# Tile starts modulo 64 bytes, chosen for each use, in a two-layer trunk

## The chip, the core and the metric
The kernel runs on one core of one Trainium2 chip. The metric is the time of one execution on the device in microseconds (us), smaller being better. TensorE multiplies matrices: it loads one operand as weights (stationary) and streams the other through (moving). VectorE (DVE) and ScalarE (ACT) work element by element, and SyncE (SP) issues the transfers (DMA) from the chip's memory into SBUF, the on-chip memory of 128 partitions. A tile is a block of SBUF: so many bytes in each partition, from a start address that is the same in all of them.

## The reference, cut to what matters
A trunk of two layers over 256 tokens of width 1024. Each layer has four blocks with a residual: a feed-forward block, four gated mixers, cross-attention to a memory of 256 tokens, and a second feed-forward block.

```python
def swiglu(h, w_in, w_out):
    a, b = jnp.split(h @ w_in, 2, axis=-1)
    return (jax.nn.silu(a) * b) @ w_out

for l in range(DEPTH):                                   # 2
    h = rms_norm(x, ffn1_pre_g[l])
    x = x + 0.5 * rms_norm(swiglu(h, ffn1_w_in[l], ffn1_w_out[l]), ffn1_post_g[l])
    h = rms_norm(x, mix_pre_g[l])
    u_conv, u_pool, q_nsa, kv_nsa, g_nsa, q_swa, kv_swa, u_gate = jnp.split(h @ w_in[l], splits, axis=-1)
    ...                                                  # four mixers: y_a, y_b, y_c, y_d
    merged = gates[:, :, 0] * (y_a @ w_branch[l, 0])
    for n in range(1, N_BRANCH):
        merged = merged + gates[:, :, n] * (branches[n] @ w_branch[l, n])
    x = x + rms_norm(merged @ w_out[l], mix_post_g[l])
    h = rms_norm(x, x_pre_g[l])
    x = x + rms_norm(cross_attention(h, rms_norm(mem, mem_g[l]), w_xq[l], w_xkv[l], w_xo[l]), x_post_g[l])
    h = rms_norm(x, ffn2_pre_g[l])
    x = x + 0.5 * rms_norm(swiglu(h, ffn2_w_in[l], ffn2_w_out[l]), ffn2_post_g[l])
```

## The kernel before
Every weight goes through the core once, as chunks of 1 MB (128 x 2048 numbers of 4 bytes) in a fixed order: per layer 22 chunks `f1i` and 11 `f1o` for the first feed-forward block; then the mixers' projections `qn`, `kva`, `kvb`, `pool`, `conv`, `qs`, `kvs`, gates `g0` to `g3` and branches `b0` to `b3`, and `wo`; then `xk`, `xq`, `xv`, `xo`; then `f2i` and `f2o`. `_fetch` (L303) loads a chunk in two halves into `raw` and splits each into a rounded part `hi` (ACT, L266) and a rest `lo` (DVE, L269). Activations are split in the same way, and each product is three matmuls (`mm3`, L282: high x high, high x low, low x high), all recorded on L280.

Two forms of product occur. With the weights stationary (`ws`), activations of 256 tokens stream through 128 weight columns at a time: the feed-forward input from its fourth chunk on, gates, branches, `xk`, `xq`. With the activations stationary (`xs_rows`, `tok_part`), the weights stream through: 512 columns in the feed-forward output, `wo`, `xv`, `xo`, `qn`, `kva` and `qs`, 280 in `kvb`, and 256 in `kvs` and in the first three chunks of each feed-forward input. A chunk of 512 columns makes 2 token tiles x 2 column halves x 2 row blocks x 3 products = 24 matmuls.

A chunk mostly goes into the pools `hi` and `lo` (four buffers of 4096 bytes each). At some places a chunk goes whole into other tiles that are free just then, its spares (`use_spare`, L326): `hT_spare` gives the tiles of hT (traced as `hwh`, `hwl`), `y_spare` those of y (`yw`), and two lambdas those of the mid pool (`sph`, `spl`) and of kT (`sp`). In each feed-forward block the spares serve its chunk 2 (y), and of the eleven output chunks the ninth (hT), tenth (y) and eleventh (mid pool). In the mixers, y serves the first half of `kva`; kT serves the last chunk of `wo`. `xs_rows` holds the last two or four chunks and goes through them once for each token tile.

hT (`hTh`, `hTl`) holds the normalised activations of the block that runs. The y tiles hold branch inputs (`ypair`, read by `branch_chunk`), then the merged sums `mh`, `ml` for `wo` (made in `mixer`), then the queries of the cross-attention. `mid` holds the feed-forward block's inner activations, `A` the normalised memory (`Ah`, `Al`) and then the attention's output `oT`.

Pools lie one behind the other. `phase` (L241) puts tiles of 32 bytes between groups of pools. In the program built from this kernel the tiles start at these remainders modulo 64 bytes:

| tiles | start modulo 64 |
|---|---|
| `hi`, `lo` | 0 |
| hT (and its spare; the attention's `pT`) | 32 |
| y (and its spare) | 32 |
| `mid` and the mid pool's spare | 0 |
| `Ah`, `Al`, `oT`, kT (and its spare), `xv` | 0 |

Slices taken from a tile (columns, tokens, row blocks) begin at multiples of 512 bytes in it, so they keep its remainder; those of `kvb` are 1120 bytes apart and alternate. Modulo 128, y is at 96 and hT at 32; `hi`, `lo`, `mid` and the mid pool's spare are at 0 (modulo 512, `hi` and `lo` are at 256, `mid` and the mid pool's spare at 0).

The order of the instructions comes from the order in the code, with priorities (`front`, `urgent`) and a planner that places work by its own estimates.

Of the kernel before, what the change touches and what calls it, by code (L numbers as in the profile page):

```python
# [8 lines left out]
F32R = mybir.dt.float32r  # L9
# [6 lines left out]
P = 128  # L16
D = 1024
S = 256
L = 2
NT = 2  # L20
KD = 8
# [25 lines left out]
          "x_post_g", "ffn2_pre_g", "ffn2_post_g")  # L47

CW = 2048
FG = 3000  # L50


# [83 lines left out]
def _pack(I):  # L136
    chunks = []
    for l in range(L):
        ch = {nm: iter(c) for nm, c in _layer_chunks(I, l).items()}
        for nm, n in _ORDER:  # L140
            for _ in range(n):
                a = next(ch[nm])
                if a.shape[1] < CW:
                    a = np.pad(a, ((0, 0), (0, CW - a.shape[1])))
                chunks.append(a)
# [61 lines left out]
class Trunk:  # L207
# [95 lines left out]
    def _fetch(self, pos):  # L303
        if pos >= len(self.plan) or pos in self.ready:
            return
        nm = self.plan[pos]
        n = 1120 if nm == "kvb" else CW
        with ExitStack() as ctx:
            for i in self.behind.pop(pos, ()):
                ctx.enter_context(self.tc.issue_after(i))  # L310
            ctx.enter_context(self.tc.high_priority(offset=FG))
            big = self.spare.pop(pos)() if pos in self.spare else None
            halves = []
            for i in range(2):
                if big is not None:
                    hi, lo = (b[:, i * n // 2:(i + 1) * n // 2] for b in big)
                else:
                    hi, lo = (p.tile([P, CW // 2], F32R, tag=t, name=t)[:, :n // 2]
                              for p, t in ((self.hip, "hi"), (self.lop, "lo")))
                raw = self.rawp.tile([P, CW // 2], F32, tag="raw", name="raw")  # L320
                self.nc.sync.dma_start(raw[:, :n // 2], self.w_d[pos, :, i * n // 2:(i + 1) * n // 2])
                self.split(hi, lo, raw[:, :n // 2])
                halves.append((hi, lo))
        self.ready[pos] = nm, halves
# [6 lines left out]
            self.early.setdefault(self.cur + at, []).append(self.cur + ahead)  # L331

    def hT_spare(self):
        return [self.hTp.tile([P, CW], F32R, tag="hT" + i, name="hw" + i) for i in "hl"]

    def y_spare(self):
        return [self.yp.tile([P, CW], F32R, tag="y", name="yw") for _ in range(2)]

    def chunk(self, nm, k):
        for pos in [self.cur, self.cur + 1] + self.early.pop(self.cur, []):  # L340
# [11 lines left out]
    def front(self):  # L352
        return self.tc.high_priority(offset=FG)

    def urgent(self):
        return self.tc.high_priority(offset=2 * FG)

    def load(self):  # L360
# [4 lines left out]
        self.x = [self.const.tile([P, D], F32, name="x%d" % t) for t in range(NT)]  # L365
        with self.tc.high_priority(offset=10 * FG):
            for h in range(2):
# [119 lines left out]
        return rs  # L487

    def new_hT(self, pool, tag):
        return [pool.tile([P, KD, S], F32R, tag=tag + i, name=tag + i) for i in "hl"]  # L490

    def pre(self, xs, g, pool, tag):
        hi, lo = self.new_hT(pool, tag)
# [102 lines left out]
    def ffn(self, l, which, h, nxt):  # L596
        nm = "f1" if which == "ffn1" else "f2"
        with self.tc.tile_pool(name="mid", bufs=1) as mp:
            mid = [mp.tile([P, NFF, S], F32R, name="mid%d" % i) for i in range(2)]
            self.use_spare(lambda: [mp.tile([P, CW], F32R, tag="sp" + i, name="sp" + i) for i in "hl"], 32, 28)  # L600
            self.use_spare(self.y_spare, 2)
            self.use_spare(self.y_spare, 31, 26)
            self.use_spare(self.hT_spare, 30, 24)

            def glu(a, b, n=S):
                t, u = self.t2([P, n]), self.t2([P, n])
                with self.front():
                    self.act(t, a, AF.Tanh, scale=0.5)
                    self.stt(u, t, 1.0, a, ALU.add, ALU.mult)
                    self.stt(t, u, 0.5, b, ALU.mult, ALU.mult)  # L610
                return t

            ws = [self.chunk(nm + "i", KD) for _ in range(3)]
            for t in range(NT):
                tok = slice(t * P, (t + 1) * P)
                vs = []
                for c in ((0, 1), (2,)):
                    ps = self.pacc((P, 2, 2, P))
                    calls = [lambda i=i, k=k: self.mm3(
                        ps[:, i - c[0]].rearrange("p a n -> p (a n)"), h[0][:, k, tok], h[1][:, k, tok],  # L620
                        ws[i][0][k], ws[i][1][k], i == c[0] and k == 0, k == KD - 1)
                        for i in c for k in range(KD)]
                    if t == 0 and c[0]:
                        self.behind_turn(calls, 2)
                    else:
                        for call in calls:
                            call()
                    v = glu(ps[:, :len(c), 0, :], ps[:, :len(c), 1, :], len(c) * P)
                    vs += [v[:, i * P:(i + 1) * P] for i in range(len(c))]
                pt = self.ptr((P, 3, P))  # L630
                for i in range(3):
                    self.nc.tensor.transpose(pt[:, i, :], vs[i], self.ident)  # L632
                self.split(mid[0][:, 0:3, tok], mid[1][:, 0:3, tok], pt)
            for i in range(3, NFF):
                w = self.chunk(nm + "i", KD)
                ps = self.pmm()
                self.ws(ps[:, 0, :], w, slice(0, P), h, KD)
                self.ws(ps[:, 1, :], w, slice(P, 2 * P), h, KD)
                v = glu(ps[:, 0, :], ps[:, 1, :])
                with self.front():  # L640
                    self.split(mid[0][:, i, :], mid[1][:, i, :], v)
            gpost = self.gain(which + "_post_g", l)
            gpre = self.gain(nxt[0], nxt[1]) if nxt else None
            hT, then = self.boundary(gpost, True, gpre)
            self.xs_rows(nm + "o", 11, lambda i, k: mid[i][:, k, :], 4, then=then)
        return hT
# [107 lines left out]
    def mixer(self, l, h):  # L754
        nc, tc = self.nc, self.tc
        with tc.tile_pool(name="mix", bufs=1) as mp:
            self.ap = mp
            self._mixer(l, h, mp)
            mg = self.merged
            mh, ml = zip(*[self.ypair() for _ in range(2)])  # L760
            for j in range(4):
                a, s2 = j // 2, slice(2 * (j % 2), 2 * (j % 2) + 2)
                with self.front():
                    self.split(mh[a][:, s2, :], ml[a][:, s2, :], mg[a][:, s2, :], scale=0.5)
        return mh, ml

    def ypair(self):

        y = self.yp.tile([P, 2, 4, S], F32R, tag="y", name="y")
        return [y[:, 0], y[:, 1]]  # L770

    def _mixer(self, l, h, mp):
        nc = self.nc
# [457 lines left out]
    def wo_cross(self, l, mg):  # L1231
        nc, tc = self.nc, self.tc
        with tc.tile_pool(name="cross", bufs=1) as cp:
# [9 lines left out]
            h, then = self.boundary(gpost, False, gpre, False)  # L1243
# [5 lines left out]
            def cols(nm, src, put):  # L1249
                for i in range(4):  # L1250
                    w = self.chunk(nm, KD)
                    ps = self.pmm()
                    for j in range(2):
                        self.ws(ps[:, j, :], w, slice(j * P, (j + 1) * P), src, KD)
                    put(i, ps)
# [10 lines left out]
                self.split(qT[0][a][:, s2, :], qT[1][a][:, s2, :], ps, scale=1.0 / 16)  # L1266

            cols("xq", h, put_q)
            pT = [self.hTp.tile([P, NT, 4, S], F32R, tag="hT" + "hl"[i], name="pT%d" % i) for i in range(2)]
            for hp in range(2):  # L1270
                for t in range(NT):
                    tok = slice(t * P, (t + 1) * P)
                    bank = self.pmm()
                    for j in range(2):
                        for dt in range(2):
                            k = (hp * 2 + j) * 2 + dt
                            a, kk = k // 4, k % 4
                            self.mm3(bank[:, j, :], qT[0][a][:, kk, tok], qT[1][a][:, kk, tok],
                                     kT[0][:, k, :], kT[1][:, k, :], dt == 0, dt == 1)
                    p = self.softmax(bank, 2, S, on_dve=True)  # L1280
# [9 lines left out]
            for hh in range(2):  # L1290
                for t in range(NT):
                    n = slice(hh * 512, (hh + 1) * 512)
                    with self.urgent():
                        self.split(v[0][:, t, n], v[1][:, t, n], acc[t][hh])
            oT = [cp.tile([P, KD, S], F32R, tag="A" + "hl"[i], name="oT%d" % i) for i in range(2)]
            for hd in range(4):
                ps = self.pmm()
                for dt in range(2):
                    n = slice((hd * 2 + dt) * P, (hd * 2 + dt + 1) * P)
# [9 lines left out]
            hT, then = self.boundary(gpost, False, gpre)  # L1309
# [10 lines left out]
def trunk_kernel(tc, x, mem, pos, stream, gains, small, consts, out):  # L1320
    with ExitStack() as ctx:
        k = Trunk(ctx, tc, x, mem, pos, stream, gains, small, consts)
        with tc.high_priority(offset=10 * FG):
            h = k.load()
# [38 lines left out]
```

## Time and profile before

| | us |
|---|---|
| median of 3 runs | 1589.12 |
| lowest and highest | 1588.38, 1589.21 |
| the profiled execution | 1588.27 |
| its span, first to last instruction | 1586.5 |
| TensorE busy in it | 1561.8 |
| DVE, ACT busy | 1148.1, 860.8 |

The profile is of one execution. TensorE's matmuls overlap: each is listed with a start and a modelled length, and the next one starts before the length is over. The distance between two starts is the time that a matmul adds. In the names, `acc<-hi,mid` is a matmul that writes `acc`, streams `hi` and has `mid` loaded as weights; numbers of buffers are left out.

### The profile page before, as it was taken

Reading aid. Unit: us, or ns where it says so; the run is one execution under the profiler, and the core shown is the slowest. Engines: PE = TensorE matmul, PEld = TensorE weight load, DVE = VectorE, ACT = ScalarE, POOL = GpSimd, SP = SyncE. Lnnn points to the kernel's source line nnn. Section 1 sums busy time; section 2 is a strip of 40 time slices with the busy share of each in tenths; the row PEclk is TensorE's granted clock in tenths of the full one; section 3 lists DMA queues with packets and bytes.
Section 4 is the critical chain, followed back from the end, with each engine's and each line's share of the span. In section 5 each row is a group of like instructions: output and inputs, shape, how many; then the busy total and the mean of one; then the engine's idle time right before and its main releaser. Section 6 shows DMA issues by size and latency. Waiting matters only on the chain.

```text
span 1586.5 us, 28413 instructions
## 1 busy us (share of the span) xinstructions
PE 1561.8 (98%) x11324; PEld 1468.4 (93%) x11324; DVE 1148.1 (72%) x1875; ACT 860.8 (54%) x1461; POOL 21.6 (1%) x44
## 2 busy tenths in 40 slices
PE   6999999999999999999999999999999999999998
PEld 6999889999998988999899987999999999899986
DVE  6666579999878576666566656799998785676653
ACT  6445455675656464545444544656755564554442
POOL 0000000000000000000000000000000000000000
PEclk9999999999999999999999999999999999999999
DMA  7555646644455554555655566465435565445562
GB/s 256 179 188 179 231 152 208 214 134 133 154 173 196 187 184 152 180 191 177 230 172 190 189 198 208 143 227 177 146 121 167 176 206 183 160 164 187 188 201 99
DMA packets 79909, 285.57 MB, mean 180 GB/s; under 512 B 8992, under 2 KB 9760, under 8 KB 79776
## 3 DMA queue, kind: packets, MB, share of 16 engines
q1 hardware_dynamic: 79776, 283.75, 54.0%
q8 instruction: 89, 1.46, 0.4%
q14 instruction: 44, 0.36, 0.1%
HBM read 282.67 MB, written 1.05 MB: 179 GB/s over the span
## 4 chain that ended last, share of the span: by engine, by line
PE 89%; DMA 4%; DVE 3%; ACT 2%; issue 1%; SPq 0%; DVEq 0%; POOLq 0%; ACTq 0%
PE mm L280 55%; PE acc L280 32%; DMA raw<-in_stream_dram 3%; ACT hi L266 1%; DVE lo L269 1%; PE tr L474 1%; PE tr L731 1%; DMA x<-in_x_dram 1%; DVE cy L277 0%; PE tr L280 0%; ACT yw L266 0%; DVE yw L269 0%; PE tr L693 0%; ACT t L266 0%; PE tr L632 0%
## 5 line engine op out<-in xcount | busy, mean ns | idle before, releaser
L269 DVE TENSOR_TENSOR lo<-raw,hi 128x1024 fp32r<-128x1024 f32 (+1 forms) x468 | 565.8, 1215 | 259.6 <-ACT hi L266 255.2
L266 ACT ACTIVATE hi<-raw 128x1024 fp32r<-128x1024 f32 (+1 forms) x468 | 489.6, 1054 | 347.6 <-PE mm L280 211.0
L280 PE MATMUL mm<-hTh,lo 128*128 128x256 f32 x2048 | 575.2, 281 | 0.0
L280 PE MATMUL mm<-hTl,hi 128*128 128x256 f32 x2048 | 573.8, 280 | 0.0
L280 PE MATMUL mm<-hTh,hi 128*128 128x256 f32 x2048 | 573.1, 280 | 0.5 <-ACT hi L266 0.5
L280 PEld LDWEIGHTS mm<-hTh,hi 128*128 128x128 f32 x2048 | 385.1, 188 | 1.1 <-ACT hi L266 0.9
L280 PEld LDWEIGHTS mm<-hTh,lo 128*128 128x128 f32 x2048 | 384.9, 188 | 0.6
L280 PEld LDWEIGHTS mm<-hTl,hi 128*128 128x128 f32 x2048 | 384.9, 188 | 0.3
L280 PE MATMUL acc<-hi,mid 128*128 128x512 f32 x512 | 156.9, 390 | 0.5 <-ACT hi L266 0.5
L280 PEld LDWEIGHTS acc<-hi,mid 128*128 128x128 f32 x512 | 96.0, 188 | 21.3 <-ACT hi L266 1.6
L277 DVE SCALAR_TENSOR_TENSOR cy<-t,sp,cy 128x256 f32<-128x256 f32 x240 | 107.9, 480 | 0.0
L266 ACT ACTIVATE mid<-t 128x256 fp32r<-128x256 f32 x76 | 31.8, 419 | 137.4 <-DVE t L277 137.4
L280 PE MATMUL acc<-lo,mid 128*128 128x512 f32 x256 | 98.0, 390 | 0.1
L280 PE MATMUL mm<-y,hi 128*128 128x256 f32 x512 | 94.1, 282 | 0.0
L280 PE MATMUL acc<-hi,hTh 128*128 128x256 f32 (+2 forms) x272 | 87.6, 323 | 1.5 <-ACT hTh L266 1.4
L280 PE MATMUL acc<-hi,hTl 128*128 128x256 f32 (+2 forms) x272 | 87.6, 322 | 1.2 <-DVE hTl L269 1.2
L280 PE MATMUL acc<-lo,hTh 128*128 128x256 f32 (+2 forms) x272 | 87.4, 322 | 0.0
L280 PEld LDWEIGHTS mm<-y,hi 128*128 128x128 f32 x512 | 79.5, 188 | 1.0
L280 PE MATMUL mm<-y,lo 128*128 128x256 f32 x256 | 72.6, 284 | 0.0
L277 DVE SCALAR_TENSOR_TENSOR t<-t,mm 128x256 f32<-128x256 f32 x160 | 66.8, 417 | 2.6
L269 DVE TENSOR_TENSOR mid<-t,mid 128x256 fp32r<-128x256 f32 x76 | 32.4, 426 | 36.9 <-ACT mid L266 36.9
L280 PEld LDWEIGHTS acc<-lo,mid 128*128 128x128 f32 x256 | 48.1, 188 | 10.8 <-DVE lo L269 1.0
(248 smaller groups left out, 2240.1 us busy)
## 6 DMA issues: line engine op xcount, KB each, us to landing
raw<-in_stream_dram SPq DMA_DIRECT2D x508, 512.0 KB, 4.4
g<-in_gains_dram SPq DMA_DIRECT2D x18, 512.0 KB, 3.8
raw<-in_stream_dram SPq DMA_DIRECT2D x8, 280.0 KB, 3.2
t<-in_mem_dram SPq DMA_DIRECT2D x4, 512.0 KB, 4.0
out_dram<-x SPq DMA_DIRECT2D x4, 256.0 KB, 2.0
x<-in_x_dram SPq DMA_DIRECT2D x2, 256.0 KB, 3.1
x<-in_x_dram SPq DMA_DIRECT2D x1, 512.0 KB, 9.3
t<-in_small_dram SPq DMA_DIRECT2D x2, 256.0 KB, 5.2
```

The lines of the kernel that those rows point to most:

```text
L266: return self.nc.scalar.activation(out, in_, func, **kw)
L269: return self.nc.vector.tensor_tensor(out, a, b, op=op)
L277: return self.nc.vector.scalar_tensor_tensor(out, a, s, b, op0=op0, op1=op1)
L280: return self.nc.tensor.matmul(out, lhsT, rhs, start=start, stop=stop, skip_group_check=True)
L474: tr = self.nc.tensor.transpose(pt[:, j, :], xn[:, j * P:(j + 1) * P], self.ident)
L731: self.nc.tensor.transpose(pt[:, j, :], s_, self.ident)
```

## The change
Tiles are made 64 bytes longer (two times `HALF`, which is 8 numbers of 4 bytes), and each use takes a slice of the tile that begins either at its start or 32 bytes into it. Since every lengthening is a multiple of 64 bytes, all tiles keep their remainder modulo 64, apart from the slices:

- Weights of `qn`, `kva`, `kvb`, `qs`, `kvs` in `hi`/`lo` begin 32 bytes into the buffer (0 becomes 32); other weights don't.
- The spare in hT begins 32 bytes in (32 becomes 0).
- The spare in y of a feed-forward block's tenth output chunk, asked for 31 chunks ahead, begins 32 bytes in (32 becomes 0); the other uses of the spare in y stay at 32.
- The merged sums `mh`, `ml` begin 32 bytes into y (32 becomes 0); the branch inputs and queries stay at 32.
- hT, A, `oT` and `pT` keep their remainder; only their tiles are longer.

```diff
+HALF = 8
...
-                    hi, lo = (p.tile([P, CW // 2], F32R, tag=t, name=t)[:, :n // 2]
+                    o = HALF if nm in ("qn", "kva", "kvb", "qs", "kvs") else 0
+                    hi, lo = (p.tile([P, CW // 2 + 2 * HALF], F32R, tag=t, name=t)[:, o:o + n // 2]
                               for p, t in ((self.hip, "hi"), (self.lop, "lo")))
...
     def hT_spare(self):
-        return [self.hTp.tile([P, CW], F32R, tag="hT" + i, name="hw" + i) for i in "hl"]
-
-    def y_spare(self):
-        return [self.yp.tile([P, CW], F32R, tag="y", name="yw") for _ in range(2)]
+        return [self.hTp.tile([P, CW + 2 * HALF], F32R, tag="hT" + i, name="hw" + i)[:, HALF:HALF + CW] for i in "hl"]
+
+    def y_spare(self, o=0):
+        return [self.yp.tile([P, CW + 2 * HALF], F32R, tag="y", name="yw")[:, o:o + CW] for _ in range(2)]
...
     def new_hT(self, pool, tag):
-        return [pool.tile([P, KD, S], F32R, tag=tag + i, name=tag + i) for i in "hl"]
+        n = KD * S
+        return [pool.tile([P, n + 2 * HALF], F32R, tag=tag + i, name=tag + i)[:, :n].rearrange("p (k s) -> p k s", k=KD)
+                for i in "hl"]
...
             self.use_spare(self.y_spare, 2)
-            self.use_spare(self.y_spare, 31, 26)
+            self.use_spare(lambda: self.y_spare(HALF), 31, 26)
             self.use_spare(self.hT_spare, 30, 24)
...
-            mh, ml = zip(*[self.ypair() for _ in range(2)])
+            mh, ml = zip(*[self.ypair(HALF) for _ in range(2)])
...
-    def ypair(self):
-
-        y = self.yp.tile([P, 2, 4, S], F32R, tag="y", name="y")
-        return [y[:, 0], y[:, 1]]
+    def ypair(self, o=0):
+
+        y = self.yp.tile([P, CW + 2 * HALF], F32R, tag="y", name="y")
+        return [y[:, a:a + 4 * S].rearrange("p (k s) -> p k s", k=4) for a in (o, o + 4 * S)]
...
-            pT = [self.hTp.tile([P, NT, 4, S], F32R, tag="hT" + "hl"[i], name="pT%d" % i) for i in range(2)]
+            pT = [self.hTp.tile([P, CW + 2 * HALF], F32R, tag="hT" + "hl"[i], name="pT%d" % i)[:, :CW]
+                  .rearrange("p (t h s) -> p t h s", t=NT, h=4) for i in range(2)]
...
-            oT = [cp.tile([P, KD, S], F32R, tag="A" + "hl"[i], name="oT%d" % i) for i in range(2)]
+            oT = self.new_hT(cp, "A")
```

## Rows read from the trace of the kernel before

**Rows 1.** The page: engines' busy us, and TensorE's granted clock by slices.
```profile
PE 1561.8 (98%) x11324; PEld 1468.4 (93%) x11324; DVE 1148.1 (72%) x1875; ACT 860.8 (54%) x1461; POOL 21.6 (1%) x44
...
PEclk9999999999999999999999999999999999999999
```

**Rows 2.** The page: shares of the chain that ended last.
```profile
PE 89%; DMA 4%; DVE 3%; ACT 2%; issue 1%; SPq 0%; DVEq 0%; POOLq 0%; ACTq 0%
```

**Rows 3.** Timeline, TensorE, ffn1's output, layer 0: start us, us, operation, names, count.
```profile
143.11 0.39 PE L280 MATMUL acc<-hi,mid 128*128 128x512 f32 x1
...
185.29 0.40 PE L280 MATMUL acc<-hwh,mid 128*128 128x512 f32 x1
...
188.10 2.95 PE L280 MATMUL acc<-yw,mid 128*128 128x512 f32 x12
190.89 0.40 PE L280 MATMUL acc<-sph,mid 128*128 128x512 f32 x1
...
193.61 0.39 PE L280 MATMUL acc<-lo,mid 128*128 128x512 f32 x1
```

**Rows 4.** Timeline, TensorE, second token tile of `wo`, layer 0, and xk's start.
```profile
497.73 2.96 PE L280 MATMUL acc<-sp,y 128*128 128x512 f32 x12
500.53 0.63 PE L280 MATMUL acc<-hi,y 128*128 128x512 f32 x2
...
502.86 2.96 PE L280 MATMUL acc<-sp,y 128*128 128x512 f32 x12
505.66 0.28 PE L280 MATMUL mm<-Ah,hi 128*128 128x256 f32 x1
```

**Rows 5.** Timeline, TensorE, part of `xv`, layer 0: 33 matmuls between these.
```profile
571.60 0.40 PE L280 MATMUL acc<-hi,Ah 128*128 128x512 f32 x1
...
579.10 0.60 PE L1284 MATMUL tr<-ident,pp 128*128 128x128 f32 x4
```

**Rows 6.** Timeline, TensorE, `qn` and `kva`, layer 0: 12 and 10 matmuls between these.
```profile
214.59 0.40 PE L280 MATMUL acc<-hi,hTl 128*128 128x512 f32 x1
...
217.39 0.39 PE L280 MATMUL acc<-yw,hTl 128*128 128x512 f32 x1
...
219.71 0.40 PE L280 MATMUL acc<-hi,hTl 128*128 128x512 f32 x1
```

**Rows 7.** Timeline, TensorE, `xk`, layer 0: the first break, 37 matmuls after its start.
```profile
510.09 0.60 PE L474 MATMUL tr<-ident,t 128*128 128x128 f32 x4
```

**Rows 8.** Timeline, TensorE, four feed-forward inputs: long runs' starts, and three ends.
```profile
38.91 0.37 PE L280 MATMUL mm<-hTl,hi 128*128 128x256 f32 x1
...
635.42 0.36 PE L280 MATMUL mm<-hTh,lo 128*128 128x256 f32 x1
...
737.47 0.40 PE L280 MATMUL acc<-hi,mid 128*128 128x512 f32 x1
...
822.30 0.36 PE L280 MATMUL mm<-hTh,hi 128*128 128x256 f32 x1
...
924.23 0.40 PE L280 MATMUL acc<-hi,mid 128*128 128x512 f32 x1
...
1416.51 0.36 PE L280 MATMUL mm<-hTh,lo 128*128 128x256 f32 x1
...
1519.54 0.39 PE L280 MATMUL acc<-hi,mid 128*128 128x512 f32 x1
```

**Rows 9.** Groups by line, DVE: busy us, mean ns of one, idle time before.
```profile
L269 DVE TENSOR_TENSOR lo<-raw,hi 128x1024 fp32r<-128x1024 f32 (+1 forms) x468 | 565.8, 1215 | 259.6 <-ACT hi L266 255.2 <-PE tr L731 2.2 <-PE mm L280 1.1
...
L269 DVE TENSOR_TENSOR yw<-raw,yw 128x1024 fp32r<-128x1024 f32 x24 | 28.9, 1222 | 6.9 <-ACT yw L266 6.7
```

**Rows 10.** Timeline, TensorE, last gate and branch, layer 0: 36 and 24 matmuls.
```profile
465.95 0.28 PE L280 MATMUL mm<-hTh,hi 128*128 128x256 f32 x1
...
470.16 0.40 PE L280 MATMUL mm<-y,hi 128*128 128x256 f32 x2
...
473.00 0.71 PE L474 MATMUL tr<-ident,t 128*128 128x128 f32 x5
```

## The prediction, made before the changed kernel ran
> **What bounds the kernel now.** I read the page's busy shares first, then the chain of work that ended last, then the order of time on TensorE, matmul by matmul. TensorE is busy 98% of the span and its granted clock is in the top tenth in every slice [rows 1]; it is 89% of the chain, DMA 4%, DVE 3%, ACT 2% [rows 2]. So the end is set by how fast matmuls follow one another. The printed length of a matmul (0.39 us at 512 columns) is no help, because matmuls overlap; what counts is the step from one start to the next. In the timeline the operand named first after the arrow streams through (moving), the second is loaded as weights (stationary). I take two starts with nothing else between them and divide by the number of matmuls.
>
> The step depends on which tiles are read. In ffn1's output projection of layer 0, `hi`/`lo` against `mid` run from 143.11 to 185.29, 186 matmuls: 226.8 ns each. Then come the spare in hT (`hw`) and the spare in y (`yw`), 12 matmuls each, from 185.29 to 190.89: 5.60 us for 24, 233.3 ns. Then the spare in the mid pool (`sp`), 2.72 us for 12: 227 ns again [rows 3]. It is the same loop with the same shapes and stationary tiles, all within some 50 us. What differs is the start modulo 64 bytes: `hi`, `sp` and `mid` are at 0, `hw` and `yw` at 32. I write a pair as (moving, stationary). At 512 columns (0,0) steps at 227 and (32,0) at 233.
>
> Of (0,32), the projection `wo` tells: `sp` against merged y takes 2.80 us for 12, 233.3 ns, and `hi` against y 2.33 us for 10, 233.0 ns [rows 4]. A few stages later the same weight tiles against A, (0,0), take 7.50 us for 33: 227.3 ns [rows 5]. For (32,32) there is one place at 512 columns: the first half of `kva` in y against hT. It takes 2.32 us for 10, 232.0 ns, where `hi` against hT just before, (0,32), takes 2.80 us for 12, 233.3 ns [rows 6]. So at 512 columns only (0,0) is cheap, by some 6 ns, and (32,32) is hardly better than (0,32).
>
> At 256 columns it is otherwise: xk, A against hi at (0,0), takes 4.43 us for 37, 119.7 ns [rows 4, 7], and hT against hi at (32,0) 116.8 to 117.9 [rows 3, 8]. The change leaves those pairs where they are.
>
> **The change part by part.**
> *Spares in ffn output chunks.* The hT spare goes from 32 to 0, and so does the y spare that is used 31 chunks ahead. Each serves one chunk of 24 matmuls (2 token tiles x 2 column halves x 2 k x 3 products) in four ffns: 192 together, all on TensorE's path. 192 x (233.3 - 227.0) = 1.21 us [rows 3].
> *Merged sums.* `mh` and `ml` go from 32 to 0, which turns all of `wo` from (0,32) to (0,0): 4 chunks x 24 x 2 layers = 192 matmuls, from 233.2 to 227.3 ns: 192 x 5.9 = 1.13 us [rows 4, 5].
> *Projection weights.* `qn`, the second half of `kva`, and `qs` go from (0,32) to (32,32): 5 chunks x 24 x 2 layers = 240 matmuls of 512 columns. By the only row of this pair they win 233.3 - 232.0 = 1.3 ns at most and, since one start rounded otherwise takes nearly that away, 0 at least: 0 to 0.3 us, of which I take 0.1 [rows 6]. `kvs`, 96 matmuls of 256 columns, has no row that I take; at the same 0 to 1.3 ns it wins up to 0.12 us, and I take 0.05. `kvb` has slices of 280 columns, 1120 bytes, which alternate between 0 and 32 before and after: nothing.
> *What pays for it.* No instruction, DMA or wait is added or taken away. DVE writes at 32 as fast as at 0: 1222 ns into `yw`, 1215 into `lo`, whose mean holds some shorter chunks [rows 9]. The padding moves other tiles by multiples of 64 bytes. The first half of `wo`'s spare comes to share 128 bytes with one gate buffer; its second half shares with four of them already, so no later wait arises.
> *Where the gain could stop.* Where weights come late, as the DMA share of the chain says [rows 2], TensorE would only wait longer. But the spares are loaded ahead of those waits, and a DMA starts when its buffer comes free, so it moves along with TensorE. At worst I put half of the gain lost, 1.2 us.
>
> Sum: 1.21 + 1.13 + 0.1 + 0.05 = 2.5 us. The profiled execution took 1588.27, of it 1586.5 span; the 1.8 us around the span stay. It would become 1585.8. The median of the runs, 1589.12, lies 0.85 above the profiled one; with the gain taken off the median: **1586.6 us**, 0.16% less.
>
> A rule speaks against the whole change: the Trainium skill (TensorE: Matmul & The Clock Gate, Step-by-step: what each phase is for) says that TensorE has two independent SBUF read ports and that "Loading the next tile's weights doesn't steal SBUF read bandwidth from the running matmul". By that rule it is of no account where a tile starts, and the sum is 0. The trace disagrees, with 227 against 233.3 ns in one loop [rows 3].
>
> **The rivals.**
> *1. The long runs change their step by themselves.* In the four ffn input projections the same pair, (32,0), settles into one of two steps: 104.20 us for 884 matmuls, 117.9 ns, in ffn1 of layer 0, and 103.03 us for 874, 117.9, in ffn2 of layer 1; but 102.05 us for 874, 116.8, in ffn2 of layer 0, and 101.93 for 873, 116.8, in ffn1 of layer 1 [rows 3, 8]. At 1.1 ns that is 0.97 us a stage. The change gives none of their tiles another remainder, but the step into which a run falls may hang on how it is entered, and entries move. Two stages can lose 0.97 each, two can win it; the runs shown spread by 0.83 us, about one such stage. Downward by one: 1585.6, by two: 1584.7; upward by two: 1588.5.
> *2. Only the difference of the remainders counts.* Then (32,32) is as good as (0,0), and the 240 projections win 5 ns more than by their row, 1.2 us: 1585.4. For it: the only row of this pair is a run of 10, which may be too short to settle. Against it: its 232.0 [rows 6].
> *3. More address bits count, and the new stride costs.* All `hi` and `lo` buffers now start 4096 bytes apart, alike modulo 128. After the change they stand 4160 apart and alternate between 0 and 64 modulo 128, and hTl moves from 32 to 96. 6144 matmuls have hT moving against them. The branch tile y, at 96 modulo 128, steps as moving operand at 2.84 us for 24, 118.3 ns, against hT's 4.21 us for 36, 116.9 ns, just before [rows 10]. If half of the 6144 came to pay these 1.4 ns, it would cost 4.3 us: 1590.9, slower. It decides from 0.8 ns on (2.5 us / 3072). At xk's 119.7, 2.8 ns more, it costs 8.6 us: 1595.2. Against it: the branch runs are 24 long and may owe their step to that, and `hi` and `sp`, which stand at different remainders of 512, step alike [rows 3].
> *4. It doesn't do what it says*, or starts are of no account, as by the rule above: no change, 1589.1. The steps of [rows 3 to 5] stand against it.
>
> **How the numbers follow.** About 0.2%, 3.2 us, is what a measurement of this kernel can tell from no change; the forecast is 0.7 us short of it. The forecast, with the long runs' steps about as they are: 0.48, of which 0.03 falls past the bound to faster. Rival 1 downward 0.16, faster; upward 0.08, same. Rival 2: 0.13, faster. Rival 3: 0.08, half of it past the bound to slower (the larger price) and half within. Rival 4: 0.05, same. 0.02 is left for a slower case that I don't see. So faster 0.32, same 0.62, slower 0.06. The range goes from rival 1 downward by two, with some of rival 2 on top, 1584.3, to a little over no change, 1589.5; rival 3 and the last part of rival 2 with rival 1 stay outside.
>
> **What would show it.** Right: `hw` and `yw` against `mid`, and all of `wo`, at 227 ns; `hi` against hT at 512 columns at 232 to 233; ACT, DVE and DMA as before. Rival 1: a run of hT against hi at the other of its two steps. Rival 2: the projections at 227. Rival 3: hT against hi at 118 or more in all four ffns and in the gates. The prediction is wrong if `wo` stays at 233, or if TensorE gets new waits.

## The result and the profile after

The changed kernel is slower: 1598.59 us (median of 6 runs, 1598.16 to 1599.42) beside 1589.2 us before (6 runs on the same chip, 1588.38 to 1591.53). The ratio is 1.0062, 95% interval 1.0051 to 1.0072. Its profiled execution took 1598.16 us, of it 1596.4 span, so 9.9 us more than the profiled one before. The prediction had 1586.6 us, 2.5 us less than before.

The page of the changed kernel, busy time by engine, granted clock, and the shares of the chain that ended last:

```profile
PE 1573.8 (99%) x11324; PEld 1478.4 (93%) x11324; DVE 1148.8 (72%) x1875; ACT 860.4 (54%) x1461; POOL 21.5 (1%) x44
...
PEclk9999999999999999999999999999999999999999
...
PE 92%; DMA 2%; DVE 2%; ACT 2%; issue 1%; SPq 0%; DVEq 0%; POOLq 0%; ACTq 0%
```

The count of instructions and the clock are what they were, DVE and ACT within 0.7 us; TensorE alone is busy 12 us longer [rows 1], and its share of the chain grew from 89% to 92% while that of the DMAs fell from 4% to 2% [rows 2]. So the matmuls themselves got slower, not the waits. The timeline of TensorE in ffn1's output, layer 0 (start us, length us, engine, line, operation, names, count), the place of [rows 3]:

```profile
142.91 0.40 PE L281 MATMUL acc<-hi,mid 128*128 128x512 f32 x1
...
185.99 0.39 PE L281 MATMUL acc<-hwh,mid 128*128 128x512 f32 x1
...
188.77 0.39 PE L281 MATMUL acc<-yw,mid 128*128 128x512 f32 x1
...
191.55 0.39 PE L281 MATMUL acc<-sph,mid 128*128 128x512 f32 x1
...
194.27 0.39 PE L281 MATMUL acc<-lo,mid 128*128 128x512 f32 x1
```

`hi`/`lo` on `mid`, whose remainder modulo 64 the change leaves at 0, step at 43.08 us / 186 = 231.6 ns; before it was 226.8. `hw` and `yw`, which the change moves from 32 to 0, step at 2.78 / 12 = 231.7 ns: better than 233.3, but not 227. Only `sp`, a spare in the same pool as `mid`, still has 2.72 / 12 = 226.7.

The four feed-forward inputs, the same view (884, 874, 873 and 874 matmuls of hT on `hi`/`lo`; the first one ends at 142.91 above), the place of [rows 8]:

```profile
38.46 0.36 PE L281 MATMUL mm<-hTl,hi 128*128 128x256 f32 x1
...
637.37 0.37 PE L281 MATMUL mm<-hTh,lo 128*128 128x256 f32 x1
...
741.15 0.40 PE L281 MATMUL acc<-hi,mid 128*128 128x512 f32 x1
...
826.93 0.36 PE L281 MATMUL mm<-hTh,hi 128*128 128x256 f32 x1
...
930.61 0.39 PE L281 MATMUL acc<-hi,mid 128*128 128x512 f32 x1
...
1425.29 0.37 PE L281 MATMUL mm<-hTh,lo 128*128 128x256 f32 x1
...
1529.15 0.39 PE L281 MATMUL acc<-hi,mid 128*128 128x512 f32 x1
```

Steps of 118.2, 118.7, 118.8 and 118.8 ns, where before they were 117.9, 116.8, 116.8 and 117.9. And the second token tile of `wo`, the place of [rows 4]:

```profile
498.81 0.40 PE L281 MATMUL acc<-sp,y 128*128 128x512 f32 x1
...
501.56 0.39 PE L281 MATMUL acc<-hi,y 128*128 128x512 f32 x1
...
503.88 0.40 PE L281 MATMUL acc<-sp,y 128*128 128x512 f32 x1
...
506.64 0.28 PE L281 MATMUL mm<-Ah,hi 128*128 128x256 f32 x1
```

`sp` on y: 2.75 / 12 = 229.2 ns and 2.76 / 12 = 230; `hi` on y: 2.32 / 10 = 232. The forecast was 227.3.

Summed over all matmuls by pair (moving/stationary; `hi` stands for `hi` and `lo`; the step is the mean from start to start in the trace, leaving out those over 1.25 times the median, which hold a wait; us is what the pair's whole start-to-start time changed by):

| pair, columns, count | step before | step after | us |
|---|---|---|---|
| hT/hi, 256, 6144 | 117.2 | 118.6 | +7.6 |
| hi/mid, 512, 768 | 227.0 | 231.5 | +1.7 (steps +3.4; the waits for weights in between shrank) |
| hi/A, 512, 288 | 228.1 | 231.8 | +1.2 |
| pT/xv, 256, 96 | 116.9 | 118.7 | +0.9 (steps +0.2) |
| hw and yw on mid, 512, 192 | 233.6, 232.6 | 231.5, 231.2 | -0.3 |
| hi and sp on y (`wo`), 512, 192 | 233.2, 233.3 | 231.2, 229.9 | -0.5 |
| hi/hT, 512, 240 | 232.9 | 231.3 | -0.4 |
| A/hi, 256, 384 | 119.9 | 118.8 | -0.4 |

The tiles that the change aims at did gain, 1.2 us in these rows. Of the tiles that it was not to touch, A on `hi` gained 0.4 us and the others lost 11.4 us.

### The profile page after: what moved, and what is told of

Same layout as the page of the kernel before. It is cut to its first block, busy times and chain, and to the rows that moved or that the text cites. A ratio compares the mean times of both kernels' runs of the same rounds, so it can differ in the third digit from the quotient of the medians.

```text
span 1596.4 us, 28413 instructions
## 1 busy us (share of the span) xinstructions
PE 1573.8 (99%) x11324; PEld 1478.4 (93%) x11324; DVE 1148.8 (72%) x1875; ACT 860.4 (54%) x1461; POOL 21.5 (1%) x44
## 4 chain that ended last, share of the span: by engine, by line
PE 92%; DMA 2%; DVE 2%; ACT 2%; issue 1%; SPq 0%; DVEq 0%; POOLq 0%; ACTq 0%
PE mm L281 54%; PE acc L281 35%; DMA raw<-in_stream_dram 2%; PE tr L476 1%; PE tr L735 1%; ACT hi L267 1%; DVE lo L270 1%; DMA x<-in_x_dram 1%; DVE cy L278 0%; PE tr L281 0%; ACT yw L267 0%; PE tr L697 0%; DVE yw L270 0%; ACT pp L267 0%; PE tr L636 0%
## 5 line engine op out<-in xcount | busy, mean ns | idle before, releaser
L267 ACT ACTIVATE t<-acc 128x512 bf16<-128x512 f32 (+3 forms) x56 | 27.2, 488 | 59.8 <-PE acc L281 56.6
```

The source lines that it names most:

```text
L267: return self.nc.scalar.activation(out, in_, func, **kw)
```

## The experiments

Two facts from the programs. Before, all `hi` and `lo` buffers start at 256 modulo 512, hT at 288, y at 224, `mid`, A, kT and xv at 0. After, the four `hi` buffers start at 256, 320, 384, 448, the four `lo` buffers at 0, 64, 128, 192, hTh at 288 and hTl at 352, y at 352 or 416, `mid` at 256, and so on. The order of the work on every engine is the same.

Theories: **V**, what costs is that starts vary from matmul to matmul. **D**, what counts is the distance, moving tile's start less stationary tile's, modulo a larger power of two than 64. The first four runs ask which tile carries the loss; their expectations call V by the name of S (stride) and set it against O (the shifted slices or the longer hT tiles cost). Each run stands beside a run of the kernel before on the same chip.

### The buffers' length alone, and the change without it

```diff
-                    hi, lo = (p.tile([P, CW // 2], F32R, tag=t, name=t)[:, :n // 2]
-                              for p, t in ((self.hip, "hi"), (self.lop, "lo")))
+                    hi, lo = (p.tile([P, CW // 2 + e], F32R, tag=t, name=t)[:, :n // 2]
+                              for p, t, e in ((self.hip, "hi", 16), (self.lop, "lo", 16)))
```

The kernel before with this edit alone (buffers 64 bytes longer, nothing else):

> The kernel before, with hi and lo buffers 64 bytes longer and nothing else: no slice is shifted, hT, y and A keep their length. Theory S (stride): what costs is that the weight buffers no longer start at one common remainder of larger powers of two, so the runs lose their short repeating pattern. Then hT against hi goes from 117.2 to 118.4 or more per matmul (6144 of them), hi against mid from 227.0 to about 231.5, hi against A from 228 to 231.8, and the time comes to 1597 to 1600 us. Rival O (offset slices, or the longer hT tiles, cost): nothing of that is here, so 1588 to 1590 us with 117.2 and 227.

1597.62 us, beside 1588.18 before. Timeline, the input and output of ffn2, layer 0 (874 and 186 matmuls):

```profile
638.64 0.36 PE L280 MATMUL mm<-hTh,lo 128*128 128x256 f32 x1
...
741.38 0.39 PE L280 MATMUL acc<-hi,mid 128*128 128x512 f32 x1
...
784.45 0.40 PE L280 MATMUL acc<-hwh,mid 128*128 128x512 f32 x1
```

117.6 and 231.6 ns. This one edit, which changes no remainder modulo 64, makes 9.4 us, as much as the whole loss. (Over all 6144 matmuls hT/`hi` is at 118.0, where S had 118.4 or more.) The other way round, the changed kernel with `hi` and `lo` of 4096 bytes again (and so the projection weights at 0):

```diff
-                    o = HALF if nm in ("qn", "kva", "kvb", "qs", "kvs") else 0
-                    hi, lo = (p.tile([P, CW // 2 + 2 * HALF], F32R, tag=t, name=t)[:, o:o + n // 2]
+                    hi, lo = (p.tile([P, CW // 2], F32R, tag=t, name=t)[:, :n // 2]
```

> The changed kernel, with hi and lo back at 4096 bytes and their weights at 0 for all chunks; the longer hT, y and A tiles and the shifted slices stay. Theory S with hi and lo alone guilty: hi against mid back at 227, hw, yw and wo at 227 as once forecast, hT against hi at 117.2: 1586 to 1587 us. Theory S with hT guilty too (hTl now stands 64 bytes off hTh modulo 128): hT against hi stays at 118 to 118.6 and hi against A near 230, 1592 to 1596 us. Rival O: as the changed kernel, 1597 to 1599.

1593.05 us, beside 1588.18. The same three places:

```profile
636.29 0.36 PE L281 MATMUL mm<-hTh,lo 128*128 128x256 f32 x1
...
739.31 0.40 PE L281 MATMUL acc<-hi,mid 128*128 128x512 f32 x1
...
781.52 0.40 PE L281 MATMUL acc<-hwh,mid 128*128 128x512 f32 x1
```

`hi`/`mid` is back at 42.21 / 186 = 226.9 ns. hT/`hi` is at 117.9 in all four inputs; here hTh stands 32 behind `hi` and hTl 96. The two edits don't add up (9.4 for the one alone, some 5 for the rest): each by itself brings hT/`hi` to about 118. Of the expectation, the part with hT guilty too came true in time; but `hw` and `yw` on `mid` (232.7 and 231.2) and `hi` on y (230.1) didn't come to 227.

### One side varied, by 64 and by 128

The kernel before, with only `hi`'s buffers 64 bytes longer (`lo` as before), and with only `hi`'s 128 bytes longer:

```diff
+                              for p, t, e in ((self.hip, "hi", 16), (self.lop, "lo", 0)))
```

> The kernel before, with the hi buffers 64 bytes longer and lo as before. Theory S: hi starts alternate, so hi against mid rises to 229 to 231.5 and hT against hi to 118 or more; 1594 to 1600 us. If only lengthening both, or the distance of hi to lo, mattered: 1588 to 1590.

> The kernel before, with the hi buffers 128 bytes longer and lo as before, so all keep their remainder modulo 128 and differ modulo 512 (0, 128, 256, 384). If the remainder modulo 128 is what has to be common: as the kernel before, 1588 to 1590 us, hi against mid 227. If a larger remainder has to be common (256 or 512): as with 64 bytes, 1594 to 1600 us, hi against mid 229 to 231.5.

1597.12 and 1595.11 us, beside 1588.18. hT/`hi` 118.4 and 117.4, `hi`/`mid` 230.9 and 229.7. In the second, the matmuls can be told apart by their distance modulo 256: `hi`/`mid` 228.8 ns at 0 and 231.4 at 128, hT/`hi` 116.7 at 32 and 118.8 at 160. So here the step goes with the distance even while starts vary: for D. But at 0 it is 228.8 and not 227, so variation has a price too. In the first run, where the distances are 64 apart, it is the larger part: `hi`/`mid` takes 230.3 ns at 0 beside 231.2 to 231.8 at 64, 128 and 192, and hT/`hi` 117.9 at 32 beside 118.4 to 119.3.

### The same shift for all: no variation, another distance

The kernel before with one small tile more behind the pools of `hi` and `lo`, so that hT, y, `mid`, A, kT and xv all move by 64 (128) bytes against `hi`, which stays:

```diff
         self.lop = pool("lo", 4)
         self.phase()
+        self.gap = pool("gap", 1)
+        nc_ = self.nc
+        nc_.vector.memset(self.gap.tile([P, 16], F32, name="gap"), 0.0)
```

> The kernel before with a tile of 64 bytes between the weight buffers and all that lies behind them: every hi and lo still starts at the same remainder, but hT, y, mid and A stand 64 bytes further from them. Theory V (what costs is that starts vary from one matmul to the next): nothing varies here, so 1588 to 1590 us, hi against mid 227, hT against hi 116.8 or 117.9 by run. Theory D (the distance of moving and stationary start, modulo some larger power of two, is what counts, and distances off a few good ones are dear): hi against mid 231 or more and hT against hi 118 or more, 1596 to 1602 us.

> As the run with 64 bytes, with 128. Theory V: 1588 to 1590 us, hi against mid 227. Theory D: in the run with hi buffers 128 bytes longer, matmuls at a distance of 128 modulo 256 stepped at 231.5 against 228.8 for 0 and, hT against hi, at 118.8 against 116.7; so here hi against mid at 231.5 and hT against hi at 118.8, 1598 to 1602 us.

1608.44 and 1603.02 us, beside 1588.85: dearer than the change, with every buffer 4096 bytes apart, and dearer than D had it (at most 1602). Timeline with the shift of 64, the same places:

```profile
640.38 0.36 PE L283 MATMUL mm<-hTh,lo 128*128 128x256 f32 x1
...
745.34 0.39 PE L283 MATMUL acc<-hi,mid 128*128 128x512 f32 x1
...
788.74 0.39 PE L283 MATMUL acc<-hwh,mid 128*128 128x512 f32 x1
```

120.1 and 233.3 ns. With the shift of 128, the inputs of ffn2 of layer 0 and ffn1 of layer 1:

```profile
638.08 0.36 PE L283 MATMUL mm<-hTh,lo 128*128 128x256 f32 x1
...
743.04 0.39 PE L283 MATMUL acc<-hi,mid 128*128 128x512 f32 x1
...
829.19 0.36 PE L283 MATMUL mm<-hTh,hi 128*128 128x256 f32 x1
...
932.87 0.39 PE L283 MATMUL acc<-hi,mid 128*128 128x512 f32 x1
```

120.1 and 118.8 ns at one and the same distance; the other two inputs have 117.4 and 120.1. V alone can't be the cause: nothing varies here, and the loss is larger. D stands, with the limit that one distance allows several steps, into one of which a run settles.

### The wanted moves without new strides

The kernel before with `hw`, the moved `yw`, the merged sums and xo's y spare at 0 modulo 64, while `hi` and `lo` keep 4096 bytes, hT's two halves lie in one tile 8192 bytes apart, and y is lengthened by 512 bytes:

```diff
-        return [pool.tile([P, KD, S], F32R, tag=tag + i, name=tag + i) for i in "hl"]
+        if tag == "hT":
+            t = pool.tile([P, 2 * CW + 2 * HALF], F32R, tag="hT", name="hT")
+            return [t[:, a:a + CW].rearrange("p (k s) -> p k s", k=KD) for a in (0, CW)]
...
-        y = self.yp.tile([P, 2, 4, S], F32R, tag="y", name="y")
+        y = self.yp.tile([P, CW + 128], F32R, tag="y", name="y")
...
+        t = self.hTp.tile([P, 2 * CW + 2 * HALF], F32R, tag="hT", name="hw")
+        return [t[:, a:a + CW] for a in (HALF, HALF + CW)]
...
-        self.sm = pool("sm", 12)
+        self.sm = pool("sm", 10)
```

> The useful shifts of the change without its strides: hi and lo stay 4096 bytes long (projection weights at 0), hTh and hTl are the two halves of one tile 8192 bytes apart, y tiles are 512 bytes longer, the spares in hT and y for the ffn outputs, the merged sums, and also the y spare of xo, start at 0 modulo 64. Theory V: hw, yw and sp against mid at 227, wo at 227, yw against oT at 227 to 229: 192 x 6.2 + 192 x 5.9 + 48 x 5 ns = 2.6 us less than before, 1585.6 (1584.5 to 1586.8 with the two steps of the long runs). Theory D: mid now stands 64 bytes off the distance that it had to hi (modulo 512), so hi against mid goes to 231, 768 x 4 ns = 3 us more, 1588 to 1590.

1586.11 us, beside 1588.85. The time is V's (1585.6) and not D's (1588 to 1590), but 2.7 us between two single runs proves no gain: the kernel before ranged from 1586.25 to 1591.32 in 15 runs. And the steps aren't those that V had:

```profile
633.55 0.37 PE L281 MATMUL mm<-hT,lo 128*128 128x256 f32 x1
...
735.62 0.40 PE L281 MATMUL acc<-hi,mid 128*128 128x512 f32 x1
...
778.27 0.40 PE L281 MATMUL acc<-hw,mid 128*128 128x512 f32 x1
```

`hi`/`mid`, now at distance 64, rose to 42.65 / 186 = 229.3 ns. `hw` on `mid`, forecast at 227 by V, still has 232.6; it is at distance 128. hT/`hi`, at 32 as before, stepped at 116.8 in all four inputs, which makes 2.4 us and is the settling that the prediction's rival 1 described. Better placed were y on `hi` (224 to 32: 118.3 to 117.0) and A on `hi` (0 to 192: 119.9 to 116.5).

### Everything moved together, hT alone moved to 0, and spacers by distance

The spacer tiles that already stand between the pools take a length. First one more of 64 bytes ahead of `hi`: every start changes, no distance between these tiles does.

```diff
+        self.phase(16)
         self.hip = pool("hi", 4)
```

> The kernel before with one more spacer tile of 64 bytes ahead of the hi pool: every tile of the matmuls but the constants moves by 64 bytes, so that no distance between hi, lo, hT, y, mid, A changes, while all starts do. Theory D (only the distance counts): 1588 to 1589.5, hi/mid 227.0, hT/hi 117.2. The rival M (the tiles' own starts count; the earlier runs that moved hT, y, mid alone by 64 bytes cost 20 us because hT and mid left their good places): about 1600 to 1608, hi/mid 233, hT/hi 119.9.

1587.71 us, beside 1588.27. The places:

```profile
634.17 0.36 PE L281 MATMUL mm<-hTh,lo 128*128 128x256 f32 x1
...
736.22 0.40 PE L281 MATMUL acc<-hi,mid 128*128 128x512 f32 x1
...
778.44 0.40 PE L281 MATMUL acc<-hwh,mid 128*128 128x512 f32 x1
```

116.8 and 227.0 ns: a shift of all starts by 64 bytes is of no account, and M falls. Then hT alone 32 bytes back, so that it stands at 0 from `hi`, both at 0 modulo 64:

```diff
         self.lop = pool("lo", 4)
-        self.phase()
...
-        self.phase()
+        self.phase(16)
         self.yp = pool("yp", 2)
```

> The kernel before without its first spacer tile of 32 bytes, and with the second 64 bytes long: hT alone goes from 32 behind hi to 0 (modulo 256); hi, lo, y, mid, A stay. All of hT's starts and hi's are then multiples of 64. Theory D: 256-column steps at distance 0 are the dearest seen (A on hi, 119.9), so hT/hi goes from 117.2 to 119.9: 6144 x 2.7 = 16.6 us, about 1604.5; hi/mid stays 227. Rival (a remainder of 0 modulo 64 on both sides is the cheap case, as the change's wording has it): hT/hi 117 or less, 1586 to 1589.

1604.63 us, where D said about 1604.5. From the timeline, `hw` on `mid` in ffn1 of layer 0 (12 matmuls), and ffn2's input:

```profile
187.05 0.39 PE L279 MATMUL acc<-hwh,mid 128*128 128x512 f32 x1
...
189.77 0.40 PE L279 MATMUL acc<-yw,mid 128*128 128x512 f32 x1
...
639.81 0.36 PE L279 MATMUL mm<-hTh,lo 128*128 128x256 f32 x1
...
744.76 0.40 PE L279 MATMUL acc<-hi,mid 128*128 128x512 f32 x1
```

hT/`hi` 104.95 / 874 = 120.1 ns, and `hw`/`mid`, which came to distance 0 too, 2.72 / 12 = 226.7. The same distance is among the dearest for 256 columns and the cheapest for 512. Last, the spacers at 64, 96 and 192 bytes, which puts hT and y 64 behind `hi`:

```diff
-        self.phase()
+        self.phase(16)
         self.hTp = pool("hT", 1)
...
-        self.phase()
+        self.phase(24)
         self.yp = pool("yp", 2)
         self.sm = pool("sm", 12)
-        self.phase()
+        self.phase(48)
```

> The kernel before, with its three small spacer tiles made 64, 96 and 192 bytes long instead of 32 each, and nothing else: hi and lo stay at 256 (modulo 512), hT goes to 320 (64 behind hi instead of 32), y to 320 (64 instead of 224 modulo 256), mid, A, kT and xv to 256 (0 from hi modulo 256, as before). Theory D (the step of a constant run is fixed by the distance of the moving tile's start from the stationary tile's start modulo 256; 256-column steps 119.9 ns at 0, 116.5 at 64, 119.8 at 96, 118.6 at 128 and 160, 116.5 at 192; 512-column steps 227 at 0, 229 at 64, 233 at 128 and 192): hT/hi 117.2 to 116.5 (6144 x 0.7 = 4.3 us), y/hi 118.3 to 116.5 (768 x 1.8 = 1.4 us), some 0.5 us from the spare chunks; together 1582 to 1584 beside 1588.2 to 1589. Rival V (only what varies from matmul to matmul costs, the start itself beyond the remainder modulo 64 is free): hT and y lose their odd 32 bytes, and the spares gain 1.2 us: about 1587.5. Rival M (the remainders of each address, not their difference, count): about 1587 to 1589 with steps that don't follow the distances.

1588.32 us, ratio to before 1.0002 (0.9993 to 1.0011): no gain where D had promised 4 us and more. The time is what V (about 1587.5) and M (1587 to 1589) had; the shift of 64 without variation and the common shift of all tiles speak against these two.

```profile
634.43 0.36 PE L280 MATMUL mm<-hTh,lo 128*128 128x256 f32 x1
...
737.45 0.39 PE L280 MATMUL acc<-hi,mid 128*128 128x512 f32 x1
...
779.64 0.40 PE L280 MATMUL acc<-hwh,mid 128*128 128x512 f32 x1
```

117.9 ns in all four inputs. The 116.5 had been read off A's runs, of at most 96 matmuls, and hT doesn't take it over. So a price holds for its distance and column count, but only to about 1 ns from one tile to another, and 1 ns of hT on `hi` is 6 us.

### The change's aim, placed by distance

Every 512-column pair that can be put there at distance 0, y and hT at 32 from `hi`:

```diff
+HALF = 56
...
+        self.phase(24)
         self.yp = pool("yp", 2)
+        self.sm = pool("sm", 10)
+        self.phase(24)
...
+        t = self.hTp.tile([P, 2 * CW + 64], F32R, tag="hT", name="hw")
+        return [t[:, a:a + CW] for a in (HALF, HALF + CW)]
...
+        return [self.yp.tile([P, CW + 64], F32R, tag="y", name="yw")[:, o:o + CW] for _ in range(2)]
...
+            self.use_spare(lambda: self.y_spare(HALF), 31, 26)
...
+            mh, ml = zip(*[self.ypair(HALF) for _ in range(2)])
```

> The aim of the change, placed by distance instead of by remainder modulo 64: hi, lo and their 4096 bytes as before, projection weights at offset 0; hT's two halves in one tile 8192 bytes apart, 256 bytes longer; y 256 bytes longer; hw, yw and the merged sums read from 224 bytes into their tile; sm with 10 buffers instead of 12 for the room; spacers of 32, 96 and 96 bytes. Distances modulo 256 that follow: hT/hi 32 (as before), hi/mid and hi/A 0 (as before), hw/mid and yw/mid 0 (before 32 and 224), merged sums as wo's stationary tile 0 (before 32), y/hi 32 (before 224), yw/hT 0 (before 192). Theory D, with the prices read so far (512 columns: 227 to 228 at 0 against 233; 256 columns: 117.0 at 32, 118.3 at 224, 119.9 at 0): wo 144 x 6 = 0.9 us, hw/mid 96 x 6.9 = 0.66, yw/mid 96 x 5.6 = 0.54, yw/A and sp/y 0.5, y/hi 768 x 1.3 = 1.0, yw/hT back 192 x 3 = 0.6: some 3 us less than before, 1585 to 1586 beside 1588.3, with hw/mid, yw/mid and hi/y at 227 to 228 each. Rival R (only remainders modulo 64 decide; 0 on both sides is the good case): the same for hw, yw and wo, but y/hi stays at 118.3 and yw/hT at 117: about 1586.5. Rival N (the steps move and the time doesn't, since DMA waits or chance in hT/hi's step take it): 1588 or more with the steps at 227.

1585.8 us (7 runs, 1584.09 to 1587.96) beside 1590.39 (11 runs): ratio 0.9971, interval 0.996 to 0.9983. It beats the kernel before by 0.29%. Its timeline in ffn1's output and in `wo`, layer 0:

```profile
185.78 0.39 PE L281 MATMUL acc<-hw,mid 128*128 128x512 f32 x1
...
188.50 0.39 PE L281 MATMUL acc<-yw,mid 128*128 128x512 f32 x1
...
191.22 0.39 PE L281 MATMUL acc<-sph,mid 128*128 128x512 f32 x1
...
497.01 0.39 PE L281 MATMUL acc<-sp,y 128*128 128x512 f32 x1
...
499.74 0.39 PE L281 MATMUL acc<-hi,y 128*128 128x512 f32 x1
...
502.00 0.39 PE L281 MATMUL acc<-sp,y 128*128 128x512 f32 x1
...
504.72 0.28 PE L281 MATMUL mm<-Ah,hi 128*128 128x256 f32 x1
```

`hw`, `yw` 2.72 / 12 = 226.7 ns each; in `wo` 2.73 / 12, 2.26 / 10 and 2.72 / 12, 226 to 227.5. By pairs: `hw` and `yw` on `mid` give 0.66 and 0.57 us, `hi` and `sp` on y 0.70 and 0.32, y on `hi` 1.0, `yw` on A 0.33; `yw` on hT, now at 0, takes 0.9 back. Gains 3.6, losses 0.9 in these, the size of the 3 us expected; the profiled execution's span is 2.5 us shorter (1584.0 beside 1586.5). The runs differ by 4.6 us, or 2.7 to 6.4 by the interval; what the tiles above don't account for isn't explained. Against rival R, y on `hi` came to 117.0 (R: 118.3) and `yw` on hT to 119.0 (R: 117). Rival N is out by the time.

### What the distances cost

From the runs in which no start varies (mean step in ns; distance modulo 256, moving less stationary; the kernel is named by its section: "64", "128" the shifts, "strides" the wanted moves, "0" hT at 0, "spacers", "aim" the last one):

| distance | 256 columns | 512 columns |
|---|---|---|
| 0 | 119.9 A/hi (before), 119.9 hT/hi (0) | 227.0 hi/mid, 228.1 hi/A (before), 226.7 hw/mid, yw/mid (aim) |
| 32 | 117.2 hT/hi (before), 117.0 y/hi (aim) | 233.6 hw/mid, 233.2 hi/y (before) |
| 64 | 117.5 hT/hi, 117.5 y/hi (spacers), 116.5 A/hi (64) | 229.2 hi/mid (strides), 230.3 hw/mid (spacers) |
| 96 | 119.9 hT/hi (64), 119.7 y/hi (128) | 233.4 hi/hT (128) |
| 128 | 118.6 A/hi (128) | 233.0 hi/mid, 232.2 hi/A (128) |
| 160 | 118.6 hT/hi (128) | 234.1 hi/hT (64) |
| 192 | 116.5 A/hi (strides) | 233.3 hi/mid (64), 233.1 hi/hT (spacers) |
| 224 | 118.3 y/hi (before) | 232.9 hi/hT, 232.6 yw/mid (before) |

The means of the changed kernel follow from it. Its hT meets `hi` at 32, 96, 160 and 224 in equal parts: the mean of 117.2, 119.9, 118.6 and 118.3 is 118.5, and 6144 x (118.5 - 117.2) = 8.0 us; measured 7.6. `hi` meets `mid` at 0, 64, 128 and 192: the mean of 227.0, 229.2, 233.0 and 233.3 is 230.6; measured 231.5.

Matmul by matmul the table doesn't hold there. In the changed kernel's trace `hi`/`mid` steps at 230.9, 232.1, 231.9 and 231.1 ns at the distances 0, 64, 128 and 192, and hT/`hi` at 118.0, 119.0, 118.2 and 119.2 at 32, 96, 160 and 224. With four distances mixed, a matmul at a good one pays nearly as much as the others: 4 ns more at 0 than where all are at 0. And the kernel with longer buffers alone mixes the same four distances of hT and `hi`, with 118.0 ns where the sum gives 118.5. At 256 columns the sum of prices is thus good to some half ns, 3 us over hT on `hi`; that it comes within 0.4 us of the changed kernel is in part luck.

That a step depends on the matmuls before it can be seen in the kernel "spacers", where `sp` on `mid`, at distance 0, follows `yw` at 64 (ffn1's output, layer 0):

```profile
190.60 0.40 PE L280 MATMUL acc<-sph,mid 128*128 128x512 f32 x1
...
192.92 0.39 PE L280 MATMUL acc<-spl,mid 128*128 128x512 f32 x1
...
193.37 0.39 PE L280 MATMUL acc<-lo,mid 128*128 128x512 f32 x1
```

The first ten take 2.32 us, 232 ns each, and only the last two 0.45 us, 225 each. Before, the twelve at this place took 226.7 ns each [rows 3].

## Why the prediction was wrong

**What bounds the kernel** held: the time went where the steps went, with no instruction added and the waits for weights, if anything, shorter.

**The step that failed** is one sentence under "what pays for it": "The padding moves other tiles by multiples of 64 bytes", costed at nothing, as was "The change leaves those pairs where they are". They are left where they are modulo 64, but not modulo 256, and the buffers' length alone cost 9.4 us. The forecast gain of 2.5 us became a loss of 9.4 us, of it 7.6 in hT on `hi` (117.2 to 118.6 ns, 6144 matmuls), a pair costed at nothing. That 64 is all that counts was taken over from the way the change is worded; the one row that spoke against it, y on `hi` at 118.3, stood in rival 3 and was set aside.

**Rival 3 was the right mechanism** and had 0.08. What it named as its sign came: hT on `hi` at 118 or more in all four inputs, and at 118.6 (before 117.0) in the shorter runs, to which the gates belong. Its prices, 1.4 and 2.8 ns for half of 6144, gave 1590.9 and 1595.2; measured were 1.4 ns for all 6144, and on top of that 4.5 ns for `hi`/`mid`, which it left out. Both of its counter-arguments failed. On "the branch runs are 24 long and may owe their step to that": with y moved from 224 to 32 the same short runs step at 117.0 instead of 118.3. "`hi` and `sp`, which stand at different remainders of 512, step alike": true, but against `mid` these stand at 256 and at 0. They speak against a period of 512 for this pair and say nothing on 128 or 256.

**The terms for the spares and `wo`** were right in size and wrong in condition. Forecast 1.21 and 1.13 us; the change gave 0.3 and 0.5, since `hw`, `yw` and merged y got to 0 modulo 64 but to distances like 64, 128 and 192 modulo 256. At distance 0, in the last experiment, they gave 1.23 and 1.02.

**Projections**: 0.1 forecast, 0.4 measured for `hi` on hT at 512 columns. Rival 2's sign, 227, didn't come. Its rule, that only the difference counts, fits: (32,32) steps at 231.3 where (0,0) steps at 231.5 in the same kernel, and moving all tiles together by 64 changed nothing. But the difference counts modulo more than 64.

**Rival 1** exists but didn't decide: at distance 32 the four inputs stepped at 116.8 or 117.9 in several kernels, which is worth 2.4 us between the kernel before and the two in which all four took 116.8. In the changed kernel all four are above both steps.

**The rule of the Trainium skill** (TensorE: Matmul & The Clock Gate, Step-by-step: what each phase is for) says that loading the next weights doesn't steal read bandwidth from the running matmul. The prediction concluded from it that starts are of no account, which the Trainium skill doesn't say. That conclusion fails: 1608.44 against 1588.85 us by one small tile that does nothing but shift, and here the measurement decides. Whether the two reads take bandwidth from each other no run shows.

**What stays open.** Why 0 is good for 512 columns and bad for 256 isn't shown; that the two reads of SBUF get in each other's way would fit, but no run looks at that. A period of 128 is out at 512 columns (227.0 at 0, 233.0 at 128). For 256 there are distances 256 apart that step alike: `hi` on `mid` at 256 before and at 0 in "spacers", 227.0 both; A on `hi` in the same two kernels, 119.9 and 119.8. Which of several steps a run settles into at one distance isn't known. How much of the changed kernel's loss is due to the distances and how much to their mixing isn't told apart, since no run varies the starts among good distances alone. The tables are from one trace a kernel, and most experiments are one run, where differences below some 5 us, the range of the kernel before, rest on the steps and not on the time; the two with intervals are named.

## What to carry to other kernels

When tiles are lengthened or moved, list the starts of every pair that TensorE reads together, moving less stationary, modulo 256, before and after; a padding that is harmless for the tile it serves shifts all that lie behind it. Keep buffers of one pool at strides that are multiples of 256, and set distances by spacers; in this kernel the good ones were 0 for 512 columns of these 4-byte numbers, and 32 or 64 for 256 columns. And test the modulus of an observed rule before costing a side effect at nothing: two pairs that agree exclude only the periods that tell them apart.

## What was not expected of the hardware

- A shift of 64 bytes between moving and stationary tiles, made by one small spacer tile, cost 19.6 us of 1588.85 (1.2%): 120.1 instead of 117 ns at 256 columns, 233.3 instead of 227 at 512.
- The cheapest distance for 512 columns (0: 226.7 to 228 ns) is, with 96, the dearest for 256 (119.9).
- A common shift doesn't matter: all tiles moved by 64 bytes together, 1587.71 beside 1588.27 us.
- With four distances mixed, matmuls at a good one lose it: `hi`/`mid` at 0 takes 230.9 ns in the changed kernel, 227.0 before.
- At one distance, runs of some 870 equal matmuls settle into different steps: 117.4, 118.8 and 120.1 ns at distance 160, 116.8 and 117.9 at 32.
